# Layer 0's first feed-forward product as seven block products, and the modulation sums moved into the second product

## The chip, the cores and the metric

The kernel runs on one core of one Trainium2 chip. The metric is the device time of one execution in microseconds, and less is better. The core's engines work at the same time: TensorE (PE; its weight loads are shown as PEld), VectorE (DVE), ScalarE (ACT), GpSimd (POOL) and SyncE (SP), which here issues all DMA transfers, in the order of one queue.

## The reference

Two layers, run on 256 context tokens and 1024 latent tokens of width 1024, in float32:

```
for l in range(2):
    sh1, sc1, g1, sh2, sc2, g2 = split(silu(cond) @ w_ada[l] + b_ada[l], 6)   # one row for each of two streams
    out = mixer(x * (1 + sc1) + sh1)          # attention, RG-LRU and chunk gMLP side by side, then w_out
    x   = LN(ALPHA * x + g1 * out; ln1)
    h2  = x * (1 + sc2) + sh2
    f   = relu(h2 @ w_ff1[l] + b_ff1[l])**2 @ w_ff2[l]      # 1024 -> 4096 -> 1024
    x   = LN(ALPHA * x + g2 * (f + b_ff2[l]); ln2)
```

`w_ada[l]` is 1024 x 6144: the modulations of a layer are a product of two condition vectors with 25 MB of weights.

## The kernel before

**Precision.** An operand of a product is split into two parts, `hi` and `lo = x - hi`, each a tile of its own (`split`, L163 to L173: the `hi` copy on ACT, the `lo` subtraction on POOL or DVE). A product is three matmuls, hi*hi, hi*lo and lo*hi (`mm3`, L177 to L179).

**Order.** The code is written with a tile framework. It derives the waits, and it orders each engine's instructions itself, by when it estimates them to be ready, with the order of the code as priority. `keep` pins an instruction behind the one that the code put just before it on the same engine. Tiles come from pools by tag: `u` (30 slots of 4 KB a partition), `x` (here 14 slots, NX), `m` (8 slots), and eight PSUM banks (`ps`). A tile that finds no free slot waits for one.

**Stages of a layer.** `in_proj`, `attention`, `out_proj`, then `ff`. In the profile the first feed-forward product of layer 0 takes about 737 to 1205 us, that of layer 1 about 2278 to 2710 us; the second product follows each of them.

**First product, plain form** (`ff1`, all 16 chunks of layer 0, and chunk 0 (C0 = 1) of layer 1). A chunk is 256 of the 4096 columns, as two weight tiles m = 0, 1. Tokens come in groups A and B (512 latent tokens each) and C (256 context tokens). For each group and m, eight k-blocks by three matmuls fill a bank, and ACT applies bias and relu. That makes 96 matmuls of 512 columns and 48 of 256 for a chunk. The last pair of tokens (group C) is turned into `h2` late (`run_late`), in layer 1 ahead of B's second tile, in layer 0 ahead of C.

**First product, seven form** (`first_seven`; layer 1, chunks 1 to 15; `SL` lists the layers that use it). The 1024 latent tokens, the k-range and the 256 columns are each cut in halves, and the 2x2 block product is made from seven block products instead of eight: seven times 12 matmuls of 512 columns, and C's 48 of 256 as before. Combinations of `h2` blocks are made once (`hstep`: `hr` loaded from a DRAM copy, `comb`, `hsplit`). Combinations of weight blocks are made for every chunk in `witem` (numbers j = 0 to 7 of a chunk): four subtractions on POOL (L1529 to L1534), eight ACT casts and eight `lo` subtractions on POOL. `WLA` says by how many products `witem` runs ahead. Products are added into the output tiles by DVE straight from PSUM (`add`, L1557), the first copied by ACT (L1579).

**Beside it.** `mid_store` forms the combinations that the second product needs, four DVE subtractions of 128x640 for each of chunks 0 to 11 (L1450 to L1453). `residual` scales the first layer norm's output, two DVE operations of 128x1024 (L1394, L1395) for each of ten blocks, one block per chunk. In layer 0 only, `ada_bg` computes 14 half-parts of modulations in the background: for each, 16 DVE operations of 128x512 accumulate `w_ada` rows times the condition (L487 the first two, L489 the other 14), then a split (ACT and POOL), four matmuls with a column of ones (L498, `sel`), a copy from PSUM and two to four small DMAs. `tick(us)` in `ff1` hands a background generator `us * rate` units (`ABR` = 0.62); a DVE operation takes 0.6 units.

**Second product** (`seven`, 42 products of 30 matmuls in each layer, `prep(n)` two ahead of `run(n)`), also by seven block products, POOL and DVE making the `lo` parts.

Of the kernel before, what the change touches and what calls it, by code (L numbers as in the profile page):

```python
# [41 lines left out]
SL = (1,)  # L42
C0 = 1
WLA = 4
# [12 lines left out]
ABR = 0.62  # L57
# [22 lines left out]
class Kern:  # L80
# [391 lines left out]
    def ada_bg(self, l, parts):  # L472
# [3 lines left out]
        for part in parts:  # L476
            for h in range(2):
                acc = self.u([P, 2, 512], s="aacc")
                c0 = part * D + h * 512
                for k in range(8):  # L480
                    if k % 2 == 0:
                        sl2 = self.u([P, 2, 512], s="aslab")
                        nc.sync.dma_start(out=sl2, in_=I["w_ada"][l, k * P:(k + 2) * P, c0:c0 + 512].rearrange("(k p) n -> p k n", p=P))
# [7 lines left out]
                hi, lo = (self.u([P, 2, 512], F32R, s="aspl") for _ in range(2))  # L491
                self.split(hi, lo, acc)
                del acc
                yield 3.0
                b = self.ps(s="ada")
                for s in range(2):
                    for w in (hi, lo):
                        nc.tensor.matmul(b[0:2, :], self.sel[:, s, :], w[:, s, :], start=s == 0 and w is hi, stop=s == 1 and w is lo)  # L498
                del hi, lo
                row = self.u([2, 2, 512], s="arow")  # L500
                if part in (2, 5):
                    nc.sync.dma_start(out=row[:, 0, :], in_=I["b_ada"][l:l + 1, c0:c0 + 512].partition_broadcast(2).squeeze(1))
                    nc.vector.tensor_tensor(row[:, 1, :], b[0:2, :], row[:, 0, :], ALU.add)
                    nc.sync.dma_start(out=self.gates[l][part // 3, :, h * 512:h * 512 + 512], in_=row[:, 1, :])
                else:
                    nc.vector.tensor_copy(row[:, 1, :], b[0:2, :])
                    nc.sync.dma_start(out=self.rows[:, h * 512:h * 512 + 512], in_=row[:, 1, :])
                    m = self.mod[l][:, part, :, h * 4:h * 4 + 4]
                    for s in range(2):
                        nc.sync.dma_start(out=m[:, s], in_=self.rows[s:s + 1, h * 512:h * 512 + 512].rearrange("o (k p) -> p (o k)", p=P))  # L510
                    yield 3.0
                    bias = self.pfm[l][:, C_BADA + part * 8 + h * 4:C_BADA + part * 8 + h * 4 + 4]
                    nc.vector.tensor_tensor(m, m, bias.unsqueeze(1).to_broadcast([P, 2, 4]), ALU.add)
                del row
                yield 0.7
# [66 lines left out]
    def run(self):  # L582
# [8 lines left out]
        for l in range(DEPTH):  # L591
            if l:
                self.x_open(NI)
                for tag in ("lg", "tp"):
                    self.ps(tag=tag, bufs=2)
# [13 lines left out]
    def cst_load(self):  # L609
# [32 lines left out]
        self.rows = self.DR.tile([2, D], F32, name="rows")  # L642
        self.hr = {l: self.DR.tile([2, 2, P, 4, 512], F32, name=f"hr{l}") for l in SL}
# [739 lines left out]
    def residual(self, l, alloc):  # L1383


        nc, I = self.nc, self.I
        st = {}

        def step(i):
            if i == 0:  # L1390
                st["g"], st["b"] = (self.bc_row(I[k][l:l + 1], "a" + k[-1], ALPHA, alloc=alloc) for k in ("ln1_g", "ln1_b"))
            if "r" in st:
                r = st.pop("r")
                nc.vector.tensor_tensor(r, r, st["g"], ALU.mult)  # L1394
                nc.vector.tensor_tensor(r, r, st["b"], ALU.add)  # L1395
                nc.sync.dma_start(out=self.rx1[l][BLOCKS[i - 1]], in_=r)
            if i < len(BLOCKS):
                r = st["r"] = alloc(s="rn")
                nc.sync.dma_start(out=r, in_=self.xn1[l][BLOCKS[i]])
            else:  # L1400
                st.clear()

        return step
# [53 lines left out]
    def first_seven(self, l, h):  # L1457
# [27 lines left out]
        def comb(e, dst, a, b, op):  # L1485
            for i in range(2):
                e.tensor_tensor(dst[i], a[i], b[i], op)
# [28 lines left out]
        def witem(n):  # L1516
# [23 lines left out]
            self.split(w[:, 0], w[:, 1], src)  # L1540
# [10 lines left out]
        def run(c, after):  # L1551
# [6 lines left out]
            def prod(j):  # L1558
# [6 lines left out]
                if j not in (0, 1, 6):  # L1565
                    del W[8 * c + j]
                if c == NCH - 1:
                    del H[j]
                return b

            def ctx(m, items):
# [5 lines left out]
                relu(f[m][:, :, 512:640], cb[:, m, :].rearrange("p (h n) -> p h n", h=2), m)  # L1577

            nc.scalar.copy(q[1, 0], prod(0))  # L1579
            add(q[0, 0], prod(1), q[1, 0])  # L1580
            relu(q[0, 0], q[0, 0], 0)
            add(q[1, 0], prod(2), q[1, 0])
            ctx(0, (0, 1))
# [184 lines left out]
    def ff(self, l, h2, fs):  # L1768
# [5 lines left out]
        residual = self.residual(l, self.x if l in SL else self.u)  # L1774
        for c in range(NCH):
            if l == 0 and c == 1:
                self.add_bg(itertools.chain(self.ada_bg(0, (5,)), self.ada_bg(1, (0, 1, 2, 3, 4, 5))), ABR)

            def after(g):
                if fs and c < C0:  # L1780
                    if c == 0 and g == "A":
                        fs["wait"](8 * C0 + 4)
                    fs["h"]((c, "ABC".index(g)))
                    if c == C0 - 1 and g != "C":
# [9 lines left out]
            if fs and c >= C0:  # L1794
                fs["run"](c, prep)
            else:
                self.ff1(l, c, h2, after)
            if 2 <= c <= 2 + len(BLOCKS):
                residual(c - 2)
# [3 lines left out]
        gb = {}  # L1803
        for n in range(7 * NQ):
            prep(n + 2)
            if n == 7 * NQ - 2:
# [3 lines left out]
        acc = result()  # L1810

# [173 lines left out]
```

## Time and profile before

| | |
|---|---|
| median of three runs | 3170.68 us (3168.12 to 3173.48) |
| the profiled execution's own time | 3168.49 us |
| its span, first to last instruction | 3166.7 us |
| PE, DVE, POOL, ACT busy | 94%, 72%, 48%, 47% of the span |
| mean granted TensorE clock | 0.977 of full speed |

The page's section 1 gives busy time of each engine; where nearly every microsecond of a stretch is PE's, the other engines' work is hidden behind it. The profiled execution lies 2.2 us under the median.

### The profile page before, as it was taken

The page shows a single profiled execution, that of the slowest core. Times are in us where ns is not written, and L with a number is a line of the kernel's source. Part 1 is how long each engine was busy: PE and PEld are TensorE (multiplying, and loading weights), DVE is VectorE, ACT ScalarE, POOL GpSimd, SP SyncE. Part 2 cuts the span into 40 slices and gives each one's busy share as a digit, 9 for nine tenths or more (in the row PEclk, how much of TensorE's full clock was granted, in tenths as well). Part 3 has the DMA queues.
Part 4 walks back from the last instruction along what each step waited for, and adds up shares of the span by engine and source line. Part 5 has one row for each costly group of instructions (what it writes and reads, how often), then busy time and mean ns, then how long its engine had stood idle before and what let it go on. Part 6 is the DMA issues. An engine that isn't in the chain of part 4 may idle for free. (4 is left out here: it accounts for less than half of the span.)

```text
span 3166.7 us, 42762 instructions
## 1 busy us (share of the span) xinstructions
PE 2974.4 (94%) x15828; PEld 2489.0 (79%) x15828; DVE 2285.9 (72%) x4529; ACT 1478.4 (47%) x2289; POOL 1521.0 (48%) x850
## 2 busy tenths in 40 slices
PE   7888999999999999999989889999989999999993
PEld 4677789788888888888767878897878888888882
DVE  8779899765666634878763989996755552587889
ACT  5554578744332324333166537894444444433301
POOL 3222244502322326857643213456557676685775
PEclk9999999999999999999999999999999999999996
DMA  6321000225666654443321100003445554544331
GB/s 228 120 89 55 15 1 8 74 97 192 220 215 231 207 181 157 153 141 115 114 103 34 52 27 7 1 23 131 168 139 179 178 181 151 178 155 138 115 110 66
DMA packets 168768, 375.83 MB, mean 119 GB/s; under 512 B 21048, under 2 KB 62792, under 8 KB 168560
## 3 DMA queue, kind: packets, MB, share of 16 engines
q1 hardware_dynamic: 168560, 373.11, 35.1%
q8 instruction: 124, 2.03, 0.3%
q14 instruction: 84, 0.69, 0.1%
HBM read 266.03 MB, written 107.02 MB: 118 GB/s over the span
## 5 line engine op out<-in xcount | busy, mean ns | idle before, releaser
L173 POOL TENSOR_TENSOR wlo<-stg,whi 128x1024 fp32r<-128x1024 f32 (+2 forms) x118 | 243.1, 2072 | 373.4 <-ACT whi L169 345.8
L177 PE MATMUL ps<-hh,whi 128*128 128x512 f32 (+1 forms) x1072 | 390.7, 365 | 14.8 <-ACT htmp L573 13.2
L178 PE MATMUL ps<-hl,whi 128*128 128x512 f32 (+1 forms) x1072 | 388.0, 362 | 4.0 <-POOL hl L393 2.2
L179 PE MATMUL ps<-hh,wlo 128*128 128x512 f32 (+1 forms) x1072 | 387.0, 361 | 0.0
L179 PE MATMUL ps<-wh,ml 128*128 128x512 f32 x840 | 334.3, 398 | 0.0
L177 PE MATMUL ps<-wh,mh 128*128 128x512 f32 x840 | 330.7, 394 | 0.7 <-DVE accy L1729 0.7
L178 PE MATMUL ps<-wl,mh 128*128 128x512 f32 x840 | 330.6, 394 | 0.0
L173 POOL TENSOR_TENSOR pt<-ptf,pt 128x512 fp32r<-128x512 f32 x128 | 166.5, 1301 | 241.3 <-DVE pt L171 225.4
L173 DVE TENSOR_TENSOR ml<-mf,mh 128x1280 fp32r<-128x1280 f32 x84 | 170.2, 2027 | 121.7 <-ACT mh L169 115.8
L177 PEld LDWEIGHTS ps<-hh,whi 128*128 128x128 f32 x1072 | 203.3, 190 | 49.4 <-ACT htmp L573 13.7
L169 ACT CAST mh<-mf 128x1280 fp32r<-128x1280 f32 x84 | 106.4, 1266 | 279.2 <-PE ps L178 233.4
L178 PEld LDWEIGHTS ps<-hl,whi 128*128 128x128 f32 x1072 | 203.8, 190 | 38.9 <-POOL hl L393 4.0
L1165 DVE TENSOR_SCALAR_CACHE_REDUCE S<-sc 128x512 f32<-128x512 f32 (+1 forms) x416 | 224.9, 584 | 11.4 <-PE pT L1176 9.5
L179 PEld LDWEIGHTS ps<-hh,wlo 128*128 128x128 f32 x1072 | 204.3, 191 | 34.5 <-issue 0.2
L173 POOL TENSOR_TENSOR wl<-wraw,wh 128x1024 fp32r<-128x1024 f32 x60 | 170.8, 2856 | 117.1 <-ACT wh L169 116.9
L1168 ACT ACTIVATE S<-S,anm 128x1280 f32<-128x1280 f32 (+1 forms) x160 | 191.2, 1196 | 37.9 <-DVE anm L1167 35.7
L1176 PE MATMUL pT<-ident,S 128*128 128x128 f32 x1344 | 201.9, 273 | 2.0 <-DVE pt L1185 1.4
L1201 PE MATMUL o<-pt,vt 128*128 128x256 f32 x1024 | 191.9, 302 | 9.6 <-POOL pt L173 7.8
L178 PEld LDWEIGHTS ps<-wl,mh 128*128 128x128 f32 x840 | 157.7, 188 | 40.1
L177 PEld LDWEIGHTS ps<-wh,mh 128*128 128x128 f32 x840 | 157.7, 188 | 38.9 <-DVE accy L1729 1.6
L179 PEld LDWEIGHTS ps<-wh,ml 128*128 128x128 f32 x840 | 157.7, 188 | 37.2
L173 POOL TENSOR_TENSOR w1s<-w1r,w1s 128x512 fp32r<-128x512 f32 x90 | 118.6, 1334 | 111.2 <-ACT w1s L169 111.2
(394 smaller groups left out, 8488.8 us busy)
## 6 DMA issues: line engine op xcount, KB each, us to landing
mf<-mc SPq DMA_DIRECT2D x84, 640.0 KB
mc<-s SPq DMA_DIRECT2D x48, 640.0 KB
aslab<-in_w_ada SPq DMA_DIRECT2D x56, 512.0 KB
stg<-in_w_ff SPq DMA_DIRECT2D x50, 512.0 KB
wraw<-in_w_ff SPq DMA_DIRECT2D x48, 512.0 KB
mc<-f SPq DMA_DIRECT2D x72, 320.0 KB
w1r<-in_w_ff SPq DMA_DIRECT2D x30, 512.0 KB
stg<-in_w_in SPq DMA_DIRECT2D x28, 512.0 KB
```

What stands on the lines that cost most here:

```text
L169: nc.scalar.copy(hi, src)
L173: e.tensor_tensor(lo, src, hi.bitcast(F32), ALU.subtract)
L177: mm(out, lh, rh, start=start, stop=False)
L178: mm(out, lh, rl, start=False, stop=False)
L179: mm(out, ll, rh, start=False, stop=stop)
L1165: nc.vector.tensor_scalar(S[:, c0:c0 + n], b[:, :n], 1.0, -3.0e38, ALU.mult, ALU.max, accum_out=u["m"][:, hh, i:i + 1])
L1168: nc.scalar.activation(S[:, :c0], S[:, :c0], AF.Exp, bias=u["nm"][:, hh:hh + 1], accum_out=u["d"]["den"][:, ci % 2, hh:hh + 1])
L1176: nc.tensor.transpose(b[:, c, hh, :], u["S"][hh][:, (2 * j + c) * P:(2 * j + c + 1) * P], self.ident)
L1201: nc.tensor.matmul(o, v, pt[:, hl, c, :], start=j == 0 and c == 0 and hl == 0, stop=j == last and c == 1 and hl == 1)
```

## The change

- `SL` becomes (0, 1): layer 0's chunks 1 to 15 also use the seven form, with a DRAM copy `hr` of its `h2`, and its late pair goes ahead of B's second tile.
- `ada_bg` keeps only the 16 DVE operations of a half-part and stores the accumulator to DRAM (`dacc`). The new `ada_red` loads it during the second product of layer 0, from n = 2 on one step for each n, and does the split (`lo` on DVE), the four matmuls, the copy and the small DMAs there. The tiles of `ada_bg` come from the `x` pool instead of `u`.
- In `run` of the seven form each of the seven products and two context parts calls `tick(2.8)`; `ABR` becomes 0.42. What is left is drained in the last chunk.
- `WLA` becomes 3. The context part of m = 0 is moved ahead of product 2. `residual` works on pairs of blocks in halves of 512 columns, with one 128x2x512 tile for gain and offset in place of two.
- `comb`, and for chunk 1 the casts and `lo` subtractions of the weights, are kept in program order. In chunk 0 the weight items are made after `hstep` of A (two) and of B (two).
- At the start of layer 1 the four `ps` banks are allocated ahead of `lg` and `tp`.

```diff
-SL = (1,)
+SL = (0, 1)
-WLA = 4
+WLA = 3
-ABR = 0.62
+ABR = 0.42
...
     def ada_bg(self, l, parts):
-                acc = self.u([P, 2, 512], s="aacc")
+                acc = self.x([P, 2, 512], s="aacc")
...
-                hi, lo = (self.u([P, 2, 512], F32R, s="aspl") for _ in range(2))
-                self.split(hi, lo, acc)
...
+                nc.sync.dma_start(out=self.dacc[l][part, h], in_=acc)
+                acc = sl = sl2 = None
+                yield 0.6
+
+    def ada_red(self, todo):
+        for l, part, h in [(l, part, h) for l, part in todo for h in range(2)]:
+            c0 = part * D + h * 512
+            acc = self.u([P, 2, 512], s="aacc")
+            nc.sync.dma_start(out=acc, in_=self.dacc[l][part, h])
+            yield
+            hi, lo = (self.u([P, 2, 512], F32R, s="aspl") for _ in range(2))
+            self.split(hi, lo, acc, lo_eng="dve")
+            yield
+            b = self.ps(s="ada")
+            for s in range(2):
+                for w in (hi, lo):
+                    nc.tensor.matmul(b[0:2, :], self.sel[:, s, :], w[:, s, :], start=s == 0 and w is hi, stop=s == 1 and w is lo)
+            row = self.u([2, 2, 512], s="arow")
...
+                self.psn = 4
+                self.ps()
...
         def comb(e, dst, a, b, op):
-                e.tensor_tensor(dst[i], a[i], b[i], op)
+                self.keep(e.tensor_tensor(dst[i], a[i], b[i], op))
...
             w = W[n] = self.x([P, 2, 4, P], F32R, s="w1s")
-            self.split(w[:, 0], w[:, 1], src)
+            if c == C0:
+                self.keep(nc.scalar.copy(w[:, 0], src))
+                self.keep(tt(w[:, 1], src, w[:, 0].bitcast(F32), ALU.subtract))
+            else:
+                self.split(w[:, 0], w[:, 1], src)
...
+                self.tick(2.8)
...
             relu(q[0, 0], q[0, 0], 0)
+            ctx(0, (0, 1))
             add(q[1, 0], prod(2), q[1, 0])
-            ctx(0, (0, 1))
...
                 if fs and c < C0:
-                    if c == 0 and g == "A":
-                        fs["wait"](8 * C0 + 4)
                     fs["h"]((c, "ABC".index(g)))
+                    if g != "C":
+                        fs["wait"](8 * C0 + (2 if g == "A" else 4))
...
+        ada = self.ada_red([(0, 5)] + [(1, part) for part in range(6)]) if l == 0 else iter(())
         for n in range(7 * NQ):
             prep(n + 2)
+            if n >= 2:
+                next(ada, None)
...
             run(n)
```

## Rows read from the trace of the kernel before

**Rows 1.** The page, section 1: busy us (share of the span) and instructions of an engine.
```profile
PE 2974.4 (94%) x15828; PEld 2489.0 (79%) x15828; DVE 2285.9 (72%) x4529; ACT 1478.4 (47%) x2289; POOL 1521.0 (48%) x850
```

**Rows 2.** Busy time by stretch: length, PE, PEld, DVE, ACT, POOL, granted clock, DMA.
```profile
758.50:771.35 12.85, 10.83 (x71) 9.87 (x70) 9.40 (x21) 5.82 (x11) 3.63 (x2) 0.87 0.60 204
771.35:1205.30 433.95, 433.95 (x2212) 360.23 (x2212) 259.92 (x320) 135.59 (x167) 118.20 (x43) 1.00 0.61 209
1205.30:1500.00 294.70, 294.36 (x1263) 236.52 (x1263) 215.50 (x246) 108.90 (x109) 214.72 (x82) 1.00 0.44 144
2307.60:2326.50 18.90, 8.87 (x48) 8.00 (x47) 17.11 (x16) 7.85 (x13) 7.08 (x3) 0.64 0.19 77
2326.50:2709.50 383.00, 381.48 (x1987) 323.49 (x1986) 180.56 (x181) 172.43 (x265) 256.90 (x178) 1.00 0.51 174
```

**Rows 3.** Groups of instructions from 771.35 to 1205.3 us (layer 0, chunks 1 to 15).
```profile
L489 DVE SCALAR_TENSOR_TENSOR aacc<-aslab,scond,aacc 128x512 f32<-128x512 f32 x194 | 156.5, 864 | 15.2 <-DMA aslab<-in_w_ada 15.2
...
L173 POOL TENSOR_TENSOR wlo<-stg,whi 128x1024 fp32r<-128x1024 f32 x24 | 71.9, 2996 | 163.9 <-ACT whi L169 161.6 <-DMA mc<-f 2.3
...
L498 PE MATMUL ada<-aspl,sel 128*2 128x512 f32 x56 | 15.2, 393 | 0.0
```

**Rows 4.** The same view from 2326.5 to 2709.5 us (layer 1, chunks 1 to 15).
```profile
L173 POOL TENSOR_TENSOR w1s<-w1r,w1s 128x512 fp32r<-128x512 f32 x87 | 114.7, 1336 | 99.6 <-ACT w1s L169 99.6
...
L1557 DVE TENSOR_TENSOR f<-ps,f 128x512 f32<-128x512 f32 x105 | 69.2, 686 | 73.6 <-PE ps L179 71.4
...
L173 DVE TENSOR_TENSOR slo<-hr,shi 128x1024 fp32r<-128x1024 f32 x6 | 9.4, 1586 | 2.6 <-ACT shi L169 2.5
```

**Rows 5.** Timeline of VectorE, 819 to 856 us: start, length, line, merged instructions.
```profile
820.30 5.39 DVE L489 SCALAR_TENSOR_TENSOR aacc<-aslab,scond,aacc 128x512 f32<-128x512 f32 x8 [0.37 <-DMA aslab<-in_w_ada]
...
839.78 0.81 DVE L1452 TENSOR_TENSOR s<-f 128x640 f32<-128x640 f32 x1
840.52 0.81 DVE L1451 TENSOR_TENSOR s<-s,f 128x640 f32<-128x640 f32 x1
...
848.19 0.88 DVE L487 TENSOR_SCALAR aacc<-aslab,scond 128x512 f32<-128x512 f32 x2 [1.41 <-DMA aslab<-in_w_ada]
...
853.60 1.23 DVE L1394 TENSOR_TENSOR rn<-rn,ag 128x1024 f32<-128x1024 f32 x1
854.86 1.23 DVE L1395 TENSOR_TENSOR rn<-rn,ab 128x1024 f32<-128x1024 f32 x1
```

**Rows 6.** Timeline of all engines around 827 us.
```profile
826.50 3.16 POOL L173 TENSOR_TENSOR wlo<-stg,whi 128x1024 fp32r<-128x1024 f32 x1 [12.74 <-ACT whi L169]
...
827.51 3.24 DVE L1395 TENSOR_TENSOR rn<-rn,ab 128x1024 f32<-128x1024 f32 x1
```

**Rows 7.** Timeline of all engines around 2443 us.
```profile
2441.88 1.88 POOL L1529 TENSOR_TENSOR w1t<-w1r,w1r 128x512 f32<-128x512 f32 x1
...
2442.53 1.91 DVE L1452 TENSOR_TENSOR s<-f 128x640 f32<-128x640 f32 x1
...
2443.84 1.76 POOL L1530 TENSOR_TENSOR w1t<-w1r,w1t 128x512 f32<-128x512 f32 x1
...
2444.37 1.91 DVE L1451 TENSOR_TENSOR s<-s,f 128x640 f32<-128x640 f32 x1
```

**Rows 8.** Timeline of GpSimd, 2344 to 2360 us.
```profile
2353.29 6.35 POOL L173 TENSOR_TENSOR w1s<-w1r,w1s 128x512 fp32r<-128x512 f32 x5
```

**Rows 9.** Timeline of all engines, 2300 to 2324 us (layer 1, end of chunk 0).
```profile
2307.37 8.26 DVE L1487 TENSOR_TENSOR hr<-hr,hr 128x1024 f32<-128x1024 f32 x5 [7.90 <-DMA hr<-hr]
...
2307.61 0.28 PE L177 MATMUL ps<-hc,whi 128*128 128x256 f32 x1
...
2315.55 6.00 DVE L577 TENSOR_TENSOR hc<-htmp,hc 128x256 fp32r<-128x256 f32 x8
...
2316.02 0.58 PE L178 MATMUL ps<-hc,whi 128*128 128x256 f32 x1 [8.14 <-DVE hc L577]
```

## Prediction before the run

> **What bounds the kernel now.** I read the page first, then busy time by stretch, then the groups of the two first products, then the timelines of the engines that the change loads. The page shows PE busy for 94% of the span [rows 1]. That is an average over stages, so the stretches decide: in layer 0's chunks 1 to 15 PE is busy for all of 433.95 us, in the second product behind it for 294.36 of 294.70 us, and in layer 1's chunks 1 to 15, which already use the seven form, for 381.48 of 383.00 us, all at full granted clock [rows 2]. In all three PE sets the pace and DVE and POOL are hidden. The reader should see one more thing there: in layer 0's stretch DVE is busy for 259.92 us and POOL for 118.20 us, in layer 1's DVE for 180.56 us and POOL for 256.90 us [rows 2]. The change puts layer 1's POOL work and layer 0's DVE work into one stretch.
>
> **Matmuls removed.** A chunk in seven form has 84 matmuls of 512 columns instead of 96. One costs 294.70 / 1263 = 0.233 us in a stretch that holds nothing else [rows 2]. 12 x 15 x 0.233 = 42.0 us less. The 56 reduction matmuls [rows 3], 13.1 us, leave the stretch too, but come back in the second product, where PE has no idle time: -13.1 and +13.1. If PE still set the pace, layer 0's chunks would take 433.95 - 42.0 - 13.1 = 378.9 us, 25.26 us each; layer 1's 383.00 us says that such a stretch can run so.
>
> **Can DVE and POOL follow?** This decides. First, the two hold each other up. A POOL subtraction that starts at 826.50 ends at 829.66; the DVE operation that starts at 827.51 takes 3.24 us, where its like takes 1.23 with POOL idle, and ends 1.1 us after POOL's [rows 5, 6]. When both have work they take turns: DVE subtractions start 1.84 us apart (2442.53, 2444.37) where alone they start 0.74 apart [rows 5, 7], so a POOL operation of 512 columns, 1.26 us alone ((6.35 - 1.30) / 4, its last one taken as 1.30) [rows 8], adds 1.10 us to DVE's queue. Operations with a PSUM input are not held: `add` has a mean of 686 ns in a stretch full of POOL work [rows 4].
> The Trainium skill ("SBUF — State Buffer", section "SBUF: two separate sides") says that a GpSimd operation and a DVE operation with two SBUF inputs take a shared port pair as an exclusive lock for the whole instruction, and that the loser fully blocks. Rows 6 agree; rows 7 show slightly less than whole durations, and by the rule taken strictly the stretch would be longer, which is the second rival below.
>
> Now count a chunk. POOL: eight `lo` parts and four combinations. DVE: `ada_bg` advances 9 x 2.8 x 0.42 = 10.6 units in a chunk, a half-part needs 16 x 0.6 + 0.6 = 10.2, so 16.6 operations a chunk, all 224 done in 13.5 chunks. 14.5 of them at 0.66 us ((5.39 - 0.74) / 7) are 9.6 us, and 2.1 at 0.40 us, 0.8 [rows 5]. Four subtractions of `mid_store` at 0.74 are 3.0, two of `residual` at 1.26 are 2.5 [rows 5]. Together 15.9 us that meet POOL's 12 x 1.10 = 13.2. Seven `add` at 0.61 (686 ns less the 0.08 by which neighbours overlap) are 4.3 us that can run while POOL holds DVE's other work. So DVE needs between 29.1 us (every `add` under a POOL operation) and 33.4 us (none), for a chunk that PE could do in 25.26. I take 30.8: POOL fits behind some 12 of DVE's 20 or so other operations, so it covers 12/20 of the `add`s.
>
> By chunks: chunk 1 has no `residual` but about half of the eight `slo` subtractions, taken at 1.26 us each for the same size, 33.3; chunk 2 28.3; chunks 3 to 11 nine times 30.8; chunk 12 without `mid_store` 27.8; chunk 13 without either 25.3. That is 391.9 us of DVE for 13 chunks in which PE has 328. PE may run ahead until its eight banks are full, some seven products and one context part, 22.5 us; chunks 14 and 15 are PE's again, 50.5 us. 391.9 - 22.5 + 50.5 = 419.9, against 433.95 now: **-14 us**, of the 55 that PE would give. Bounds: every `add` covered, 13 x 1.7 less, -36; none covered, 13 x 2.6 more, +20.
>
> **Reductions in the second product.** +13.1 us of PE, with no idle time to take them [rows 2]. DVE gets 14 `lo` parts of 1024 columns (1.59 us mean, `slo`) [rows 4] and 14 copies of about 0.7: 215.50 + 32 = 248 us of some 308. Loads, splits and matmuls of a half-part are one product apart, about 7 us, which covers a DMA and a split; small DMAs in SP's queue stand ahead of the `mf` loads, which are two products early. I take nothing more, at most +4.
>
> **Start of layer 1's seven form.** At 2307.61 PE wants the late pair's `lo`, but the scheduler put five `comb` operations, 8.26 us, ahead of those eight subtractions, and PE idles 8.14 us [rows 9]; over this stretch the granted clock averages 0.64, so part of it runs at 1.2 GHz [rows 2]. The 48 context matmuls are worth about 5.7 us (half of 0.233 plus a little), the stretch takes 18.90: 13 us lost. `keep` puts the subtractions first. What is late next are the combined blocks: products 0 and 1 and the moved context part give 8.5 us of cover, `comb` and the first two `slo` need about 8.3 + 1 + 2.4 after the pair's 3, with POOL's first weights holding DVE as above. So some returns at product 2: **-8**, between -13 and 0.
>
> **Start of layer 0's.** Now 12.85 us for 16 transposes and 48 matmuls [rows 2], at 0.12 us each 7.7, so some 5 us lost; moving the late pair hides that, the combined blocks bring their own wait. I take **0**, from -5 to +8. DRAM copies (`dacc`, 14 x 512 KB twice; `hr`, 4 MB each way) meet a DMA share of 0.61 and 0.44 [rows 2]: hidden. In SP's queue a `dacc` store waits for its accumulation, with the next weights' loads behind it; these are issued about two products before their first split, which `WLA` = 3 puts three products before PE. Cover 14 us, cost nothing; without it the stretch goes to the second rival. Bank order at layer 1's start, `residual` in halves and `WLA` keep their work: 0.
>
> **Sum.** -14 + 13 - 8 + 0 = -9 on the profiled execution's 3168.5 us: 3159.5. The median stands 2.2 us above it, so about 3162.
>
> **Rivals.**
> *Products stay dense (faster by far).* If DVE's background never delays an `add`, because PE runs far enough ahead, layer 0 gives the full 42: 3170.7 - 42 - 8 = 3121. For it: layer 1's stretch is dense with POOL busy 256.90 of 383 us. Against it: 15.9 + 13.2 us a chunk exceed 25.26 before any `add`. 0.10.
> *The lock decides (slower).* With whole durations, 12 x 1.30 + 14.5 x 0.74 + 2.1 x 0.48 + 4 x 0.81 + 2 x 1.23 = 33.0 us a chunk [rows 5, 8], 2.2 more than taken: the stretch takes 448, layer 0 loses 14 and the reductions 13, layer 1 gives 8: 3190. That is what the rule of the Trainium skill's "SBUF — State Buffer" gives. It decides from where a chunk needs 31.5 us: 0.7 x 13 = 9 more, and the sum is zero. For it: the counts; against it: rows 7 show pairs 0.16 us shorter than 0.74 + 1.26. 0.30.
> *Nothing measurable.* Layer 1's wait only moves from the context part to product 2 (0 instead of -8), the rest as forecast: 3170. Or a chunk needs some 31.5. 0.22.
> *The forecast,* 3150 to 3164: 0.38.
>
> **How the numbers follow.** About 0.2%, 6.3 us, is what a measurement here tells from no change. Faster takes the forecast and the dense case, 0.48; same 0.22; slower 0.30. The best bounds (-36 + 13 - 13) give 3135, the worst that I weigh (+20 + 13 + 0 + 4) 3208; leaving a tenth on either side, the range is 3132 to 3198. The forecast's own range is 3150 to 3164.
>
> **What would show it.** In the changed trace, layer 0's chunks 1 to 15 take near 420 us with PE busy below 95% and waiting on `add`; L489's mean is well above 864 ns [rows 3], POOL's weight operations above 1336 [rows 4]; chunks 14 and 15 are dense. The second product is near 308 us, still dense. Layer 1's idle time at the context part is gone, with a shorter wait at product 2. The prediction is wrong if PE is dense in layer 0 (then it is 3121), or if PE's granted clock there is under 1.00 or PE waits for weights (`w1s`) rather than banks: then SP's queue or the `x` slots, not DVE, hold it.

## The result and the profile after

The changed kernel takes 3216.14 us (median of 4 runs, 3212.69 to 3223.02) against 3169.4 us (4 runs, 3166.2 to 3173.48) for the kernel before: a ratio of 1.0146, interval 1.0132 to 1.0159. It is slower, where the forecast was 3162 us with a range up to 3198. The profiled execution took 3217.2 us with a span of 3215.4.

Busy time by stretch of the kernel after; the columns are those of [rows 2]. The stretches are layer 0's chunks 1 to 15, its second product, layer 1's chunk 0, and layer 1's chunks 1 to 15:

```profile
771.30:1242.40 471.10, 410.87 (x1981) 339.32 (x1980) 397.17 (x407) 173.63 (x262) 302.14 (x180) 0.93 0.61 212
1242.40:1560.20 317.80, 309.34 (x1319) 240.47 (x1318) 268.62 (x288) 126.38 (x128) 217.81 (x83) 1.00 0.49 163
2333.70:2372.40 38.70, 34.92 (x162) 28.82 (x160) 21.35 (x37) 15.73 (x27) 8.26 (x6) 0.87 0.52 185
2372.40:2759.00 386.60, 382.41 (x1983) 322.70 (x1982) 185.03 (x184) 178.44 (x268) 268.33 (x183) 1.00 0.49 171
```

By stretches that begin at the same matmul in both kernels, the 48.7 us of the two spans are: layer 0's chunks 1 to 15 471.2 instead of 434.1 (+37.1), its second product 317.8 instead of 294.6 (+23.2), chunk 0 of layer 0 -3.0, chunks 0 to 15 of layer 1 together 425.3 instead of 425.1, the tail behind layer 0's second product -9.8, the rest +1.1.

In layer 0's chunks PE was dense before [rows 2]; now it is busy for 410.87 of 471.10 us at a mean granted clock of 0.93. That accounts for the stretch: 378.9 us of dense matmuls (the prediction's own figure), 60.2 idle, and 61.4 us in which the record of the granted clock shows 1.2 GHz, half of it lost, 30.7; together 469.8. (PE's busy time exceeds the 378.9 by 32.0, near these 30.7.) The same three terms, with the matmuls that the kernel in question has there, close within 5 us for every kernel below.

What PE waited for there (waiting line, what ended the wait, us in total, times, longest):

```profile
PE ps L177 <- ACT w1s L169: 22.5, 9, 5.4
PE ps L179 <- POOL w1s L173: 16.8, 15, 2.7
PE psc L177 <- ACT f L1585: 11.6, 3, 5.5
PE ps L179 <- POOL w1s L1567: 8.9, 1, 8.9
```

Three of these lines, 48.2 us, are waits for weights (`w1s`). The third, 11.6 us, is a wait for a PSUM bank: the context parts of a chunk share one bank, and PE's write of the second half waits until ACT has read the first (L1585, `f<-psc`). These three stops stand in chunks 12, 13 and 14; the longest:

```profile
1180.33 0.47 ACT L1585 ACTIVATE f<-psc,pfm 128x256 f32<-128x256 f32 x1
...
1180.85 0.58 PE L177 MATMUL psc<-hc,w1s 128*128 128x256 f32 x1 [5.54 <-ACT f L1585]
```

But for the 8.9 us at the start of chunk 1, taken up below, both kinds go through ACT, and ACT's longest wait in the same stretch is for DVE:

```profile
ACT f L1585 <- DVE f L1586: 186.1, 44, 9.2
```

One such stop in the timelines of ACT, DVE, POOL and PE (start, length, line, operation, idle time before it):

```profile
845.17 0.73 ACT L1585 ACTIVATE f<-f,pfm 128x512 f32<-128x512 f32 x1 [4.12 <-DVE f L1586]
...
849.87 1.06 ACT L1424 ACTIVATE ag<-ag 128x1024 f32<-128x1024 f32 x1 [1.83 <-DMA ag<-in_ln_b]
851.39 0.72 ACT L1585 ACTIVATE f<-f,pfm 128x512 f32<-128x512 f32 x1 [0.47 <-DVE f L1586]
852.02 0.46 ACT L1585 ACTIVATE f<-psc,pfm 128x256 f32<-128x256 f32 x1
852.38 0.61 ACT L169 CAST w1s<-w1t 128x512 fp32r<-128x512 f32 x1
...
840.39 4.14 DVE L490 SCALAR_TENSOR_TENSOR aacc<-aslab,scond,aacc 128x512 f32<-128x512 f32 x3
844.46 0.68 DVE L1586 TENSOR_TENSOR f<-ps,f 128x512 f32<-128x512 f32 x1
...
847.60 0.83 DVE L1475 TENSOR_TENSOR s<-f,f 128x640 f32<-128x640 f32 x1 [0.35 <-ACT f L1628]
...
850.67 0.69 DVE L1586 TENSOR_TENSOR f<-ps,f 128x512 f32<-128x512 f32 x1
...
853.06 1.28 POOL L173 TENSOR_TENSOR w1s<-w1t,w1s 128x512 fp32r<-128x512 f32 x1 [9.74 <-ACT w1s L169]
...
853.04 0.79 PE L177 MATMUL ps<-shi,w1s 128*128 128x512 f32 x1 [5.39 <-ACT w1s L169]
```

Read it from the bottom. PE stood 5.39 us for a `hi` cast, POOL 9.74 us for the same. The cast (852.38) stands in ACT's queue behind the activation at 851.39. That one needs DVE's `add` at 850.67, which stands in DVE's queue behind the four subtractions of `mid_store` that begin at 847.60, and these began only when ACT had squared `f` (L1628). ACT was late with that because its activation at 845.17 had waited 4.12 us for the `add` at 844.46, which stood behind three accumulations that take 1.4 us each while POOL works. A load that ACT needed (849.87) adds 1.83 us. From 843.33 on POOL is idle, so the hold makes the first of these delays, and the order of the queues carries it on. The matmul at 853.04 takes 0.79 us where its like takes 0.39: PE resumes at half clock.

The groups of DVE and POOL in that stretch that answer to [rows 3, 4]:

```profile
L490 DVE SCALAR_TENSOR_TENSOR aacc<-aslab,scond,aacc 128x512 f32<-128x512 f32 x196 | 212.2, 1131 | 10.9 <-DMA aslab<-in_w_ada 10.9
...
L173 POOL TENSOR_TENSOR w1s<-w1r,w1s 128x512 fp32r<-128x512 f32 x84 | 136.3, 1636 | 93.3 <-ACT w1s L169 79.1 <-DVE aacc L490 14.2
```

An accumulation takes 1131 ns instead of 864, a `lo` part on POOL 1636 instead of 1336.

### The profile page after: what moved, and what is told of

Its sections match the earlier page's. It is cut to its first block, busy times and chain, and to the rows that moved or that the text cites. A ratio compares the mean times of both kernels' runs of the same rounds, so it can differ in the third digit from the quotient of the medians.

```text
span 3215.4 us, 43217 instructions
## 1 busy us (share of the span) xinstructions
PE 2968.2 (92%) x15648; PEld 2472.4 (77%) x15648; DVE 2483.8 (77%) x4654; ACT 1537.0 (48%) x2410; POOL 1709.0 (53%) x988
## 5 line engine op out<-in xcount | busy, mean ns | idle before, releaser
L173 POOL TENSOR_TENSOR w1s<-w1r,w1s 128x512 fp32r<-128x512 f32 x168 | 245.9, 1478 | 139.3 <-ACT w1s L169 125.1
L173 POOL TENSOR_TENSOR wlo<-stg,whi 128x1024 fp32r<-128x1024 f32 (+2 forms) x88 | 161.3, 1848 | 196.4 <-ACT whi L169 176.9
L1585 ACT ACTIVATE f<-f,pfm 128x512 f32<-128x512 f32 x120 | 86.7, 723 | 295.0 <-DVE f L1586 294.5
L1586 DVE TENSOR_TENSOR f<-ps,f 128x512 f32<-128x512 f32 x210 | 139.6, 684 | 113.1 <-PE ps L179 90.5
L173 DVE TENSOR_TENSOR ml<-mf,mh 128x1280 fp32r<-128x1280 f32 x84 | 177.8, 2117 | 62.8 <-ACT mh L169 51.6
L490 DVE SCALAR_TENSOR_TENSOR aacc<-aslab,scond,aacc 128x512 f32<-128x512 f32 x196 | 212.2, 1131 | 10.9 <-DMA aslab<-in_w_ada 10.9
L179 PE MATMUL ps<-shi,w1s 128*128 128x512 f32 x480 | 198.6, 414 | 22.1 <-POOL w1s L173 13.1
L177 PE MATMUL ps<-shi,w1s 128*128 128x512 f32 x480 | 196.7, 410 | 21.5 <-ACT w1s L169 21.5
L178 PE MATMUL ps<-slo,w1s 128*128 128x512 f32 x480 | 195.8, 408 | 3.1 <-DVE slo L173 3.1
L178 PEld LDWEIGHTS ps<-wl,mh 128*128 128x128 f32 x840 | 157.7, 188 | 37.1
```

Of the source, the lines that this page charges most:

```text
L173: e.tensor_tensor(lo, src, hi.bitcast(F32), ALU.subtract)
L177: mm(out, lh, rh, start=start, stop=False)
L178: mm(out, lh, rl, start=False, stop=False)
L179: mm(out, ll, rh, start=False, stop=stop)
L490: nc.vector.scalar_tensor_tensor(acc[:, s, :], sl, self.sc[:, k, s:s + 1], acc[:, s, :], ALU.mult, ALU.add)
L1585: relu = lambda x, y, m: nc.scalar.activation(x, y, AF.Relu, bias=bias[m])
```

## Experiments

All times in us; ratios are to the kernel before, run on the same chip. "Chunks" is layer 0's chunks 1 to 15, "second" its second product, "stopped" PE's idle time in the chunks, "half" the time there at 1.2 GHz.

```
run                  chunks second stopped half   whole    ratio, 95% interval
before                434.1  294.6    0      0   3169.4
after                 471.2  317.8   60.2  61.4  3216.14  1.0146 1.0132..1.0159
no_lock               415.3  324.9   23.8  23.9  3172.02  1.0010 0.9998..1.0021
bank_ctl              471.0  318.3   62.1  54.6  3229.06  1.0190 1.0173..1.0207
late_store            472.8  315.7   60.9  64.9  3219.04  1.0158 1.0143..1.0173
x13                   475.6  316.1   64.7  58.0  3253.48  1.0260 1.0245..1.0275
sums_only             420.8  317.3    0      0   3185.11  1.0047 1.0029..1.0065
layer1_parts          437.2  294.6    2.6    0   3170.04  0.9999 0.9990..1.0009
psum_acc              408.0  332.2   21.5  23.9  3181.46  1.0038 1.0024..1.0051
start_dve             471.0  316.3   61.6  58.0  3216.75  1.0155 1.0137..1.0172
start_lo              474.0  318.4   61.5  58.0  3229.20  1.0189 1.0172..1.0206
lookahead_4           463.8  321.1   55.3  61.4  3233.26  1.0196 1.0179..1.0214
psum_sums_first       438.0  294.6   31.6  30.7  3159.65  0.9971 0.9961..0.9981
psum_sums_first_lo    437.7  294.6   32.1  30.7  3159.05  0.9973 0.9961..0.9984
psum_sums_late        461.6  294.6   45.8  51.2  3182.25  1.0040 1.0026..1.0054
psum_sums_dve         439.6  294.6   34.1  30.7  3164.76  0.9984 0.9974..0.9993
psum_sums_dve_4       437.0  294.6   31.2  30.7  3183.57  1.0040 1.0025..1.0055
psum_sums_deferred    447.5  295.7   38.5  41.0  3172.31  1.0005 0.9996..1.0013
psum_sums_def_dve     439.4  294.6   33.6  27.3  3171.06  1.0008 0.9999..1.0017
```

**Is it the hold of DVE and POOL on each other?** `no_lock` gives each accumulation a PSUM bank in place of its second SBUF input. `bank_ctl` only takes that bank away from the products.

```diff
-nc.vector.scalar_tensor_tensor(acc[:, s, :], sl, self.sc[:, k, s:s + 1], acc[:, s, :], ALU.mult, ALU.add)
+nc.vector.scalar_tensor_tensor(acc[:, s, :], sl, self.sc[:, k, s:s + 1], self.zb, ALU.mult, ALU.add)
...
-        self.psn = 8
+        self.psn = 8 if l else 7
+        if l == 0:
+            self.zb = self.ps(s="zb", tag="zb", bufs=1)
+            nc.vector.memset(self.zb, 0.0)
```

> The changed kernel, but the 196 accumulating VectorE operations of layer 0's background take a zeroed PSUM bank as their second input in place of the accumulator (the modulations of layer 1 are then not computed; the loads, stores, tiles and the count of operations stay; one PSUM bank fewer for products in layer 0). Theory 1, VectorE and GpSimd hold each other up on operations with two SBUF inputs: these operations now leave GpSimd alone, so layer 0's chunks 1 to 15 fall from 471 us to 390 to 410 and the whole to about 3145 (3130 to 3160). Theory 2, the weights wait for free x slots and behind stores in SyncE's queue, whoever holds them: the stretch stays above 450 us and the whole above 3195.

> The changed kernel with one PSUM bank fewer for products in layer 0 (seven in place of eight), nothing else: the control for the run without the two-input operations. Theory 1 and theory 2 both expect the time of the changed kernel, 3216 us, within 6 us, since TensorE waited for weights there and not for banks. If it is over 3225, banks count.

The same number of DVE and POOL instructions of the same sizes takes 55.9 us less, and one bank fewer changes nothing in the chunks (471.0). Neither whole lies where it was expected: `no_lock` has 3172 instead of 3130 to 3160, 415.3 in the chunks instead of 390 to 410 and 324.9 in the second product; `bank_ctl` has 3229 instead of 3216, 8.6 us of it in the tail behind the second product (134.4 instead of 125.8). DVE's group in the chunks of `no_lock`:

```profile
L490 DVE SCALAR_TENSOR_TENSOR aacc<-aslab,scond,zb 128x512 f32<-128x512 f32 x196 | 134.9, 737 | 22.5 <-DMA aslab<-in_w_ada 22.5
```

196 x (1131 - 737) = 77 us of DVE were the hold. This is the main cause of the 37.1 us that the chunks lost.

**Or SP's queue, or the `x` slots?** `late_store` issues the `dacc` store a quarter of a half-part later, behind the second load of the next one. `x13` has one slot fewer in the `x` pool.

```diff
+                        if k == 2 and pend is not None:
+                            nc.sync.dma_start(out=self.dacc[l][pend[0], pend[1]], in_=pend[2])
...
-                nc.sync.dma_start(out=self.dacc[l][part, h], in_=acc)
+                pend = (part, h, acc)
...
-NX = 14
+NX = 13
```

> The changed kernel, but the store of a finished accumulator to DRAM is issued after the second slab load of the next half-part, so that SyncE's queue need not wait for VectorE there (it waited 109 us in all); the accumulator holds its x slot somewhat longer. Theory 2 (queue and slots): the whole falls by 15 to 35 us, to 3181 to 3201. Theory 1 (VectorE and GpSimd hold each other up): within 6 us of 3216.

> The changed kernel with 13 x slots in place of 14, in both layers. Theory 2 (weights wait for slots): layer 0's chunks grow by 15 us or more, the whole above 3231. Theory 1: within 6 us of 3216, as one slot only shortens how far the weights run ahead.

Both stay near 471 in the chunks (472.8 and 475.6). But `late_store` hardly took the wait out of SP's queue. The store in the changed kernel, then in `late_store`:

```profile
SPq L492 <- DVE aacc L490: 108.9, 14, 18.0
SPq L487 <- DVE aacc L494: 99.1, 11, 17.8
```

So it doesn't decide what the queue costs. One slot fewer costs the chunks 4.4 us; what more slots would give no run shows, and the changed kernel's trace does have waits for them. ACT's casts of weights don't read this tile, they wait for its slot:

```profile
ACT w1s L169 <- DVE aacc L490: 20.1, 12, 6.4
```

The forecast's own sign, that SP's queue or the slots hold PE if it waits for weights, named the wrong main holder: `no_lock` keeps the tiles, loads and stores and is 55.9 us shorter. How much the queue and the slots add is open. `x13` goes above 3231, but not in the chunks; it loses its 37 us elsewhere: 27.0 in the tail behind the second product (152.7 against 125.7) and 13.8 at the kernel's end (175.6 against 161.8).

**Each part alone.** `sums_only` leaves layer 0 without the seven form (`SL = (1,)`) and keeps the moved sums; `layer1_parts` also puts `ada_bg` and `ABR` back as before the change.

> The changed kernel with the seven form in layer 1 alone (SL = (1,)); the sums over partitions stay in the second product, orders, banks and layer 1's start as changed. Both theories: layer 0's chunks 1 to 15 take 420 us (434 less the 56 matmuls), 51 less than changed, the second product stays at 318, so about 3165 (3155 to 3175). If it stays over 3190, the seven form of layer 0 is not what costs.

> The kernel before with only what the change does outside layer 0's seven form and the moved sums: kept orders, chunk 0's order, context part ahead of product 2, WLA 3, residual in halves, bank order. From the changed trace: 8 to 10 us less between the two layers, 4.5 less in layer 1's chunk 0, 4 to 6 more in layer 1's chunks: 3158 (3152 to 3166). If those gains came from the moved sums and not from these edits: 3166 to 3172.

`sums_only`: -13.3 in the first product, as taken, but +22.7 in the second, where +13.1 was taken; the whole, 3185, is above the 3155 to 3175 expected. `layer1_parts`: no change, so its better case (3158) failed. Layer 1's chunk 0 is 5 us shorter there (38.2 against 43.2) and its chunks 1 to 15 6 us longer (388.0 against 381.9). In the changed kernel too: behind chunk 0, PE now stops at the combined blocks and the late pair instead (window from 2325 to 2400 us):

```profile
PE ps L178 <- DVE hc L589: 3.8, 6, 1.4
PE ps L178 <- DVE slo L173: 3.1, 3, 2.0
```

**Running sums in PSUM.** `psum_acc` keeps the accumulators in two PSUM banks (six for the products) and copies them out by ACT for the store.

```diff
-                acc = self.x([P, 2, 512], s="aacc")
+                acc = [self.ps(s="acc", tag=f"acc{s}", bufs=1) for s in range(2)]
...
+                sum_ = self.x([P, 2, 512], s="aacc")
+                for s in range(2):
+                    nc.scalar.copy(sum_[:, s, :], acc[s])
...
-        self.psn = 8
+        self.psn = 8 if l else 6
```

> The changed kernel, the background's accumulators in two PSUM banks (six left for products in layer 0), copied to an x tile by ScalarE when a half-part is done and stored from there; all is computed. VectorE's accumulation then has one SBUF input, as in the run where it read a zeroed bank. Theory 1 (VectorE and GpSimd hold each other up): layer 0's chunks 1 to 15 take 400 to 418 us instead of 471, the whole 3150 to 3175. Theory 2 (x slots and queue): the accumulator's slot is also free most of the time, so a gain of the same kind is possible, but below 30 us; the run with one x slot fewer tells how much a slot is worth.

The chunks take 408.0, 63 us less than in the changed kernel. But the second product grows to 332.2, and the whole is at 1.0038 (3181, where 3150 to 3175 was expected). In the second product too this run has six banks, and of 18.4 us for which PE stops there 17.5 are waits for banks that DVE had not emptied, 5.6 of 8.5 in the changed kernel; the longest line:

```profile
PE ps L177 <- DVE accx L1763: 11.4, 7, 4.4
```

Whether the two banks make the difference was not separated.

**What the moved sums meet in the second product.** The timeline of the changed kernel, POOL and DVE, and then one tile's row (min/median/max ns):

```profile
1320.56 3.35 POOL L173 TENSOR_TENSOR wl<-wraw,wh 128x1024 fp32r<-128x1024 f32 x1 [3.94 <-ACT wh L169]
...
1321.60 2.33 DVE L526 TENSOR_TENSOR mod<-mod,pfm 128x8 f32<-128x8 f32 x1
...
L526 DVE TENSOR_TENSOR mod<-mod,pfm x8: 153/2368/2378, 1321.6 to 1504.2; 128x8 f32<-128x8 f32 x8
```

An addition of eight columns takes 2.33 us: it ends when POOL's `wl` does. The same operation had a median of 164 ns in the first product of before. With the longer `lo` parts of the sums (1921 ns instead of the 1586 of [rows 4]) DVE comes to 268.62 us instead of the 248 taken, falls behind with the adds of products, and PE, which had no idle time there, stops for 8.5 us.

**The start of chunk 1.** PE stops for 8.86 us, until 789.17. The timelines of POOL and DVE ahead of it:

```profile
773.70 14.19 POOL L1512 TENSOR_TENSOR hr<-hr,hr 128x1024 f32<-128x1024 f32 x2 [6.71 <-DVE hr L1512]
...
770.14 4.62 DVE L1512 TENSOR_TENSOR hr<-hr,hr 128x1024 f32<-128x1024 f32 x4
774.68 0.81 DVE L1475 TENSOR_TENSOR s<-f,f 128x640 f32<-128x640 f32 x1
775.42 4.62 DVE L173 TENSOR_TENSOR slo<-hr,shi 128x1024 fp32r<-128x1024 f32 x4
779.96 0.81 DVE L1476 TENSOR_TENSOR s<-s,f 128x640 f32<-128x640 f32 x1
...
787.92 4.50 DVE L173 TENSOR_TENSOR slo<-hr,shi 128x1024 fp32r<-128x1024 f32 x2 [4.55 <-POOL hr L1512]
```

POOL's two combinations take 14.19 us; at layer 1's start the same two take 6.29. Meanwhile DVE runs its row at full pace. `start_dve` moves this combination to DVE; `start_lo` makes chunk 1's `lo` weights on DVE and puts two of them ahead of the late pair.

```diff
-                comb(nc.gpsimd, s4, s4, hr["s2"], ALU.subtract)
+                comb(nc.vector, s4, s4, hr["s2"], ALU.subtract)
...
-                self.keep(tt(w[:, 1], src, w[:, 0].bitcast(F32), ALU.subtract))
+                self.keep(nc.vector.tensor_tensor(w[:, 1], src, w[:, 0].bitcast(F32), ALU.subtract))
```

> The changed kernel, the last of the four block combinations of h2 (two subtractions of 128x1024) on VectorE instead of GpSimd. In the trace the GpSimd one stood for 11.9 us behind a row of VectorE operations, the kept weight parts waited behind it and TensorE idled 8.9 us, then ran 10 us at half clock. If that is the cause of chunk 1's 40 us: layer 0's chunks shorten by 8 to 15 us, layer 1's by 2 to 6, the whole 3197 to 3206. If the combined blocks are late anyway, VectorE being the longer queue: within 6 us of 3216.

> The changed kernel, but for the weights of layer 0's chunk 1, whose lo parts are made on VectorE instead of GpSimd, and two of these weight items stand ahead of the late pair's work. Theory A (the 8.9 us gap at the start of chunk 1 and the half clock behind it come from a GpSimd operation that is held off by a row of VectorE operations with two SBUF inputs): with no GpSimd operation in that place the gap goes, layer 0's chunks 1 to 15 take 457 to 463 us instead of 471.2, the whole about 3206. Theory B (VectorE's row itself is what the start waits for): the same work in one queue is no earlier, the chunks stay within 6 us of 471 and the gap only has another name.

Neither moves the chunks (471.0, 474.0). In `start_dve` the hold only falls on the next POOL operation, a `lo` part of 512 columns:

```profile
773.62 11.84 POOL L1567 TENSOR_TENSOR w1s<-w1t,w1s 128x512 fp32r<-128x512 f32 x1 [11.34 <-ACT w1s L1566]
```

In `start_lo` PE stops for 10.7 us behind `w1s` on DVE and ACT instead (6.5 and 4.2). Theory B stands there: the row of DVE's work, with whatever POOL adds to it, is what chunk 1 starts behind.

**Does ACT's queue make it, or DVE's lateness?** `lookahead_4` sets `WLA` back to 4, so that the casts stand a product earlier in ACT's queue.

> The changed kernel with the weights of the seven form split four products ahead of TensorE instead of three (in both layers); the work of each engine is the same. Chain theory (a late add on VectorE holds ScalarE's queue, and the weights' casts behind it): the casts stand a product earlier in the queue, most of the 39 us of waits for split weights go, and layer 0's chunks take 435 to 455 us instead of 471.2. Need theory (VectorE and GpSimd simply need 32 us a chunk): the chunks stay at 465 to 475, and TensorE's waits only change their name.

463.8, just short of either: the waits for split weights did not go (24.3 on ACT's, 13.0 on POOL's, instead of 22.5 and 16.8), and layer 1's chunks lose 20 us (406.3), where PE now stops 15.0 us for the context parts' bank, 8 times. For layer 0's weights ACT's queue carries the delay from DVE to PE; a place earlier in that queue doesn't take it away. As more weights ahead also take more slots, the run doesn't test the queue alone.

**Sums back in the first product, accumulators in PSUM.** `psum_sums_first` has the accumulators of `psum_acc` (from the common ring of eight banks), no `dacc` and no `ada_red`: split (`hi` on ACT, `lo` on DVE from PSUM) and the 56 reductions are in `ada_bg` again, with `ABR` 0.46. `psum_sums_first_lo` adds `start_lo`.

```diff
+                for s in range(2):
+                    nc.scalar.copy(hi[:, s, :], acc[s])
+                    nc.vector.tensor_tensor(lo[:, s, :], acc[s], hi[:, s, :].bitcast(F32), ALU.subtract)
+                del acc
+                yield 0.6
+                b = self.ps(s="ada")
```

> The seven form in layer 0, but the sums over partitions are made where they were before the change, in the first product, and the running sums of the background stand in two PSUM banks, so that VectorE's accumulations have one SBUF input; the background's rate is 0.46 instead of 0.42, so that it ends within the stretch. Theory 1 (the two losses are VectorE's and GpSimd's hold on each other in the first product, and the moved sums in the second): layer 0's chunks 1 to 15 take 408 of the run with PSUM sums plus 13 for the 56 reductions, 421 us; the second product is back at 295 to 297; the whole 3146 to 3158. Theory 2 (two PSUM banks fewer for the products cost as much as they give, or the reductions' chain stalls the first product): the chunks take over 435 us and the whole is at or above 3168.

> The run before this one (PSUM sums, reductions in the first product) together with the lo parts of chunk 1's weights on VectorE. Theory A of the start: another 8 to 14 us less than it, 3135 to 3148 in all. Theory B: within 6 us of it.

This version beats both kernels: 3159.65 us, ratio 0.9971 (0.9961 to 0.9981), just above the 3146 to 3158 of its theory 1. The second product is back at 294.6. The chunks missed their 421 by 17 us and, at 438.0, lie where theory 2 (two banks fewer, or the reductions' chain) put them; its 3168 or more for the whole did not come. PE's waits there speak for the reductions:

```profile
PE ada L502 <- ACT aspl L495: 14.9, 7, 4.0
PE ps L179 <- POOL w1s L1558: 9.6, 2, 8.9
PE ada L502 <- DVE aspl L496: 4.7, 9, 1.1
```

19.6 us at the reductions, 11.8 for weights, all but 0.7 of it at the start of chunk 1 (9.6 on POOL, 2.2 on ACT). `psum_acc` stopped for 21.5 us, all for weights, so 10.1 of the 17 are longer stops and 3.4 more half clock. The addition of `start_lo` changed nothing.

**Can those 19.6 us be had?** Five variants of `psum_sums_first`: `psum_sums_late` waits 3.0 units between split and reductions and runs at 0.52; `psum_sums_dve` copies `hi` on DVE (1.5 units, 0.48); `psum_sums_dve_4` adds `WLA` 4; `psum_sums_deferred` issues a half-part's reductions behind the eighth accumulation of the next; `psum_sums_def_dve` does that with `hi` on DVE.

```diff
+KRED = 3
...
+                    if k == KRED and pend is not None:
+                        r, pend = red(*pend), None
+                        yield from r
...
-                    nc.scalar.copy(hi[:, s, :], acc[s])
+                    nc.vector.tensor_copy(hi[:, s, :], acc[s])
```

> The run with PSUM sums and the reductions in the first product, but between the split of a half-part's sums and its four reduction matmuls the background now waits for 3.0 units instead of 0.6, as before the change, and its rate is 0.52 instead of 0.46 so that it still ends within the stretch. Theory 2a (PE stood 19.6 us at reduction matmuls whose split was not done, and lost some 10 us more to the half clock behind those stops): layer 0's chunks take 408 to 415 us instead of 438.0, the whole 3128 to 3140. Theory 2b (two PSUM banks fewer for the products are what costs): the idle time moves from the reductions to the weights, the chunks stay over 430, the whole at 3150 to 3160.

> The run with PSUM sums and the reductions in the first product, but the hi part of the sums is copied on VectorE instead of ScalarE, so that no ScalarE queue stands between the sums and the reductions; 1.5 units instead of 0.6 between split and reductions, and a rate of 0.48. Chain theory: of the 19.6 us for which TensorE stood at the reductions 10 to 15 go, and 5 or so of half clock; layer 0's chunks take 415 to 428 us instead of 438.0, the whole 3138 to 3152. If it is VectorE's backlog alone (28 operations more there, about 17 us): 435 to 445 and the whole at 3158 to 3168.

> The run before this one with the weights split four products ahead. Chain theory: TensorE's waits for split weights go too, layer 0's chunks 405 to 425 us, the whole 3130 to 3150, with most of what is left at the start of chunk 1. Otherwise: within 5 us of the run before.

> The run psum_sums_first with the same operations and the same rate of the background, but the four reduction matmuls of a half-part are issued behind the eighth accumulation of the next half-part, some 9 us later, so that no late VectorE operation stands just ahead of them. If the 19.6 us at the reductions come from their place in TensorE's queue: they go, with some 10 us of half clock behind them; layer 0's chunks take 408 to 418 us instead of 438.0, the whole 3130 to 3142. If VectorE's load as such sets the pace: the waits turn up at the products' weights or banks, the chunks stay at 432 to 440, the whole at 3155 to 3165.

> The run psum_sums_deferred with the hi part of the sums copied on VectorE instead of ScalarE, so that neither TensorE nor ScalarE has an instruction that waits closely for an accumulation; VectorE has 28 operations more, about 17 us over the chunks. Queue theory (late accumulations hurt through the queues that wait for them): layer 0's chunks take 410 to 425 us instead of 447.5 (psum_sums_first: 438.0), the whole 3130 to 3148. Load theory (VectorE's load as such): 440 to 460 us, the whole 3165 to 3180.

All five missed their better case. In `psum_sums_deferred` PE no longer stands at the reductions, but ACT's cast of the sums stands for DVE, and PE for the weights behind it:

```profile
ACT aspl L525 <- DVE acc L516: 53.4, 10, 8.3
```

With that cast on DVE as well, 439.4 us remain. In each of these five some queue waits for a late DVE instruction, and none is shorter than `psum_sums_first` by more than 1 us. Keeping the accumulations from being held is the only edit that shortened the chunks of the seven form by more than 8 us.

## Why the prediction was wrong, step by step

**Matmuls removed: right.** -42.0 and -13.1 were there to be had. `sums_only` gave the 13.3; with the stops and the half clock the matmul terms close the account of every run within 5 us.

**Can DVE and POOL follow: the step that failed.** The hold is there as the text has it (`no_lock` and `psum_acc`), but the stretch takes 471.2 where the sum said 419.9. The text took DVE as busy without a break for 391.9 us, until the last `add` of chunk 13. That `add` ended at 1201.68, 430.5 us after chunk 1's first matmul. The columns below are those of [rows 2]. The first window goes up to it, the second holds chunks 3 to 11 (by the starts of ACT's copies of the first products, L1610), the third the part of chunk 14 that PE ran without a stop:

```profile
771.22:1201.68 430.46, 373.90 (x1796) 307.99 (x1795) 387.23 (x395) 155.57 (x236) 276.52 (x163) 0.93 0.62 213
847.48:1136.24 288.76, 255.06 (x1221) 208.49 (x1220) 261.30 (x270) 102.77 (x161) 183.19 (x112) 0.94 0.67 230
1186.14:1208.94 22.80, 22.79 (x109) 18.57 (x108) 13.19 (x14) 9.06 (x13) 16.77 (x12) 0.99 0.41 150
```

DVE's busy time, holds included, was sized well: 387.23 us against 391.9, and 29.0 us a chunk in chunks 3 to 11 against 30.8. What the sum had at nothing is 43.2 us in which DVE was idle; a chunk in the middle took 32.1 us with it. The longest of these waits, up to 1201.7:

```profile
DVE aacc L490 <- DMA aslab<-in_w_ada: 10.9, 8, 2.7
DVE rn L1412 <- DMA rn<-xn: 10.8, 4, 5.9
DVE aacc L488 <- DMA aslab<-in_w_ada: 7.0, 2, 4.0
DVE slo L173 <- POOL hr L1512: 4.5, 1, 4.5
DVE aacc L488 <- POOL w1t L1554: 4.0, 1, 4.0
```

Loads are 28.7 us of it, and DVE works in order, so the adds behind a late load were late too. No run takes these waits away (`late_store` has 20.3 us for the slabs and 12.4 for `rn`), so what they cost stays open. They are no measure of it by themselves: in `no_lock`, where less is held, DVE waits 42.5 us for the slabs and the chunks are 55.9 us shorter.

The other 12.8 us of the 51.3 lie behind that `add`: 40.8 us to the end, where the text had 50.5 - 22.5 = 28.0. The run-ahead itself was right at the end: in chunk 14 PE ran seven products and one context part, 22.8 us, until all eight banks were full (ACT's copy of the first of these products stands at 1209.62). But when DVE's last `add` of chunk 13 ended PE was only 15.5 us into that chunk, and then it stopped 3.68 us for the context parts' bank and ran 3.4 us at half clock. In chunks 1 to 11 PE didn't reach the banks: it stopped 45.0 us for weights, whose casts wait in ACT's queue for late adds. The text let PE be held by full banks alone. Seen from PE, the same loss is 60.2 us of stops and 30.7 at half clock, a term that the text had only as a sign of being wrong.

**Rivals.** "The lock decides" came nearest in time, at 3190, by 33.0 us of DVE in a chunk, where DVE was busy for 29.0; it too kept the run-ahead and full clock. By the Trainium skill ("SBUF — State Buffer", section "SBUF: two separate sides") the loser blocks for the whole instruction; the eight-column addition of 2.33 us agrees. "Products stay dense" is out.

**Reductions in the second product: mis-sized,** 13.1 taken and at most 4 more; +23.2 measured. The matmuls were nearly as taken (PE busy 309.34 us instead of 294.36 + 13.1); 8.5 us are stops. The eight bias additions, 16.7 us in all and left out of the working, are the clearest part of it.

**Start of layer 1: 0 instead of -8.** Here the rival "the wait only moves" was right, though to the product behind, in chunks 1 to 15: 425.1 and 425.3 us over both stretches, and `layer1_parts` at 426.2.

**Start of layer 0: between -5 and +8, nearly.** Chunk 0 gained 3.0 and chunk 1's start lost 8.86, +5.9 in sum; with the half of 10.2 us at half clock beside that stop it is 11.0. The last two are counted above.

**DMAs at nothing: not borne out.** DVE waited 28.7 us for loads, and `late_store`, whose store still waited 99.1 us, doesn't show that the queue costs nothing.

**Open.** The tail behind layer 0's second product is 123 to 153 us in these runs and 9.8 shorter after the change; no run tells why. What would remove the stop at chunk 1's start was not found. That the half clock is caused by the stops rests on their standing side by side in every run and on both falling together, not on a run that separates them.

## What to carry to other kernels

Before moving background work into a stretch, add up what VectorE and GpSimd do there with two SBUF inputs: a running sum kept in PSUM took 748 ns for each accumulation where it took 1131 in SBUF. Don't take the late engine as busy without a break: VectorE's work was sized within 5 us, and it was idle for 43 us more, mostly for loads. Don't credit TensorE with all its banks as a lead before looking for an in-order queue that both engines depend on; here ScalarE's, in which weights for TensorE stood behind an activation that waited for VectorE. And price a moved step by the neighbours in its new place, small operations too.

## What the runs showed of the hardware that was not expected

GpSimd can be held off for a whole row of VectorE operations, not only for one: a 512-column subtraction took 11.84 us in `start_dve` (1.26 us alone by [rows 8]), while VectorE's operations of the same 11 us ran at the durations that they have alone (1.22 and 0.81 us). Where the two take turns [rows 7], both pay instead. And an operation's size says little about its price beside GpSimd: in the second product an addition of eight columns took 2.37 us seven times of eight, and 0.15 us once.
